# A two-layer streaming encoder on one core: cross attention moves from one woven stream into the other, and the large tiles become pages of one pool

## The chip, the core and the metric

The kernel runs on one core of one Trainium2 chip. PE (TensorE) multiplies matrices, DVE (VectorE), ACT (ScalarE) and POOL (GpSimd) work on elements, and SP (SyncE) issues nearly all DMAs. Each of the five takes its instructions in the order in which they stand in its queue. The metric is the device time of one execution in microseconds; the time before is the median of three runs.

## What is computed

Two layers run over 1,024 prompt tokens and 32 sample tokens, both with the same weights. A layer of the reference, cut to its steps:

```python
z = split_in(rms_norm(x, g[N_MIX_PRE]), p['w_in'])           # one projection, 1024 -> 2720
a = diff_finish(blocked_queries(... diff_attention ...))      # 8 heads, two softmaxes each
b = band_prompt(z['b_q'], z['b_k'], z['b_v'], p['rel'])       # 4 heads, own chunk and 8 before it
c = blocked_queries(... mla_attention ...)                    # 4 heads, latent keys and values
x = x + rms_norm(concat([a, b, c]) @ p['w_out'], g[N_MIX_POST])
x = x + rms_norm(cross_attention(rms_norm(x, g[N_X_PRE]), mk, mv, w_xq, w_xo), g[N_X_POST])
f = (silu(conv(h @ w_gate)) * (h @ w_up)) @ w_down            # h = rms_norm(x, g[N_F_PRE])
x = x + rms_norm(f, g[N_F_POST])
```

The sample tokens do the same against given caches of keys and values, and the new keys, values and states are outputs as well.

## The kernel before

Activations lie transposed, 128 features on the partitions and tokens along the row. The 1,056 tokens are two halves (`HW = (544, 512)`; the 32 sample tokens belong to half 0), and each half is two groups of 256 or 288 columns. Every large product is done with three matmuls (`mm3`, L214 to L216): operands are split into a rounded high part and the rest, and high times high, high times rest and rest times high are summed. So each weight tile of 128 x 1024 is loaded into `wr`, rounded by ACT (`hi`, L112) into `wh`, and its rest taken by POOL (`lo`, L131) into `wl`; `get` runs this feed two tiles ahead, in an order that `make_feed` writes out.

The work of a half in a layer has four parts. `project` is the norm and the input projection; `attend` is the attention of groups A, B and C, whose units pass through a pipeline of steps (scores, weights, transpose, product); `cross` is the output projection w_out, the cross attention and the norms around them; `ffn` is the gated MLP, two weight tiles of w_gate and w_up to one of w_down. In names, stage(l, h) is layer l, half h. Inside `cross`, `outputs` brings in the attention's results from DRAM, the w_out loop copies its products out by ACT at L1423, and what follows is a chain: `queries` (norm, norm, w_xq, L1457), `attention` over 256 memory tokens (L1475, L1518), `rest` (w_xo, norm, the MLP's norm). The sums of squares of a norm are added by DVE and POOL at L243 and summed over partitions by a matmul with ones at L251. The MLP's first gate product is evacuated by DVE at L1585, its last sums are added at L1645.

All parts are generators, which yield the PE time that they have just issued, or a negative number for a time in which others should be issued. `weave` runs attention as the main stream with one other stream as its fill:

```python
self.weave(self.attend(0, 1), w1, tail(0, 0), tail_cost(0, 0), 350.0 / w1)
self.weave(first(1), w0, tail(0, 1), tail_cost(0, 1), 250.0 / w0)
self.weave(self.attend(1, 1), w1, tail(1, 0), tail_cost(1, 0), 350.0 / w1)
self.emit(tail(1, 1))
```

Here `tail(l, h)` is cross, ffn and the next layer's project of one half, and `first(l)` is attend(l, 0) with the sample tokens' attention spread through it. So cross(l, h) and ffn(l, h) follow each other in one stream, and the last half of the last layer runs alone. A scheduler then takes the instructions in about the order of issue, and fixes where each stands on its engine and which buffer a tile gets. Buffers come from one pool with a count for each tag: `X=16, y=8, op=4, V=3, e0=2, e1=1, s=3` for the large ones, among them X for split activations, op for keys, V for values, e for softmax weights and s for their transposes.

## Time and profile before

| | |
|---|---|
| median of 3 runs (lowest to highest) | 3822.57 us (3818.94 to 3830.19) |
| the profiled execution | 3822.06 us |
| its span, first to last instruction | 3820.3 us |
| busy in the span: PE, POOL, DVE, ACT | 3322.2, 2079.6, 2034.8, 1833.2 us |
| mean granted clock of PE | 0.921 |

Busy time is a union of an engine's instructions. The granted clock is a share of the full 2.4 GHz. A wait is put down to the work that ended last before it.

### The profile page before, as it was taken

To read this page: it belongs to the slowest core of one execution; us is meant where nothing else is said; L and a number is where in the kernel's file an instruction comes from. 1 tells how busy PE (TensorE), PEld (TensorE's weight loads), DVE (VectorE), ACT (ScalarE), POOL (GpSimd) and SP (SyncE) were. 2 spreads that over 40 slices of the span, in tenths; PEclk is the share of its full clock that TensorE was granted. 3 is DMA by queue.
4 is the path that set the end of the run, shared out by engine and by line. 5 is a ranking of instruction groups with operands and counts; after the bars stand their busy time and mean duration, and the time that the engine had idled before them with its cause. 6 is when DMAs were issued, how large, how long until landed. Compare 5 with 4: busy or idle time off the path is not lost.

```text
span 3820.3 us, 65949 instructions
## 1 busy us (share of the span) xinstructions
PE 3322.2 (87%) x24536; PEld 3138.7 (82%) x24536; DVE 2034.8 (53%) x4627; ACT 1833.2 (48%) x3926; POOL 2079.6 (54%) x1868
## 2 busy tenths in 40 slices
PE   7989977689999798778999999776999996679997
PEld 7979876589999797768999888766999996669997
DVE  4464437855555633574544543487555553554444
ACT  4464556654444535574434344565544444543332
POOL 6454455456555644545666554545655554556564
PEclk9989988899999998878999989878999998789998
DMA  7657643223233455333333365323324323122222
GB/s 243 200 173 227 213 143 105 87 79 104 82 105 107 145 197 161 121 95 100 108 96 108 97 209 187 112 75 96 105 82 122 107 90 105 61 76 91 84 89 78
DMA packets 246791, 464.78 MB, mean 122 GB/s; under 512 B 42544, under 2 KB 136136, under 8 KB 246472
## 3 DMA queue, kind: packets, MB, share of 16 engines
q1 hardware_dynamic: 244024, 457.07, 38.3%
q8 instruction: 194, 3.18, 0.4%
q0 software_dynamic: 2448, 3.51, 0.3%
q14 instruction: 125, 1.02, 0.1%
HBM read 365.93 MB, written 97.66 MB: 121 GB/s over the span
## 4 chain that ended last, share of the span: by engine, by line
PE 63%; DVE 16%; ACT 6%; DMA 5%; issue 5%; POOL 4%; SPq 1%; POOLq 0%; DVEq 0%; ACTq 0%
PE ps_g L214 17%; PE ps_g L215 17%; PE ps_g L216 17%; DVE gt L1609 3%; PE ps_g L547 2%; PE ps_g L251 2%; PE ps_g L618 1%; DVE y L441 1%; PE ps_g L617 1%; POOL wl L131 1%; ACT wh L112 1%; DVE s L129 1%; DVE X L409 1%; DVE zn L243 1%; DVE sm L690 1%
## 5 line engine op out<-in xcount | busy, mean ns | idle before, releaser
L214 PE MATMUL ps_g<-X,wh 128*128 128x256 f32 (+1 forms) x5120 | 1486.6, 292 | 34.3 <-ACT X L112 19.0
L215 PE MATMUL ps_g<-X,wh 128*128 128x256 f32 (+1 forms) x5120 | 1479.7, 290 | 8.0 <-POOL X L131 5.0
L216 PE MATMUL ps_g<-X,wl 128*128 128x256 f32 (+1 forms) x5120 | 1470.2, 288 | 1.8 <-POOL wl L131 1.8
L131 POOL TENSOR_TENSOR wl<-wr,wh 128x1024 fp32r<-128x1024 f32 x416 | 991.5, 2389 | 572.9 <-ACT wh L112 554.5
L214 PEld LDWEIGHTS ps_g<-X,wh 128*128 128x128 f32 x5120 | 982.6, 192 | 46.8 <-ACT X L112 23.7
L215 PEld LDWEIGHTS ps_g<-X,wh 128*128 128x128 f32 x5120 | 981.6, 192 | 12.7 <-POOL X L131 6.3
L216 PEld LDWEIGHTS ps_g<-X,wl 128*128 128x128 f32 x5120 | 977.2, 191 | 2.6 <-POOL wl L131 2.0
L112 ACT ACTIVATE wh<-wr 128x1024 fp32r<-128x1024 f32 x416 | 432.8, 1052 | 796.4 <-PE ps_g L215 540.4
L214 PE MATMUL ps_g<-hs,wh 128*128 128x256 f32 (+1 forms) x1424 | 412.0, 298 | 41.5 <-DVE y L1645 35.3
L215 PE MATMUL ps_g<-hs,wh 128*128 128x256 f32 (+1 forms) x1424 | 411.8, 292 | 5.6 <-POOL hs L131 5.6
L216 PE MATMUL ps_g<-hs,wl 128*128 128x256 f32 (+1 forms) x1424 | 408.9, 290 | 0.0
L640 ACT ACTIVATE e<-ps_sc,sm 128x640 f32<-128x640 f32 (+7 forms) x384 | 278.7, 727 | 139.8 <-DVE e L706 52.7
L1609 DVE SCALAR_TENSOR_TENSOR gt<-gt,cst,gt 128x32 f32<-128x32 f32 (+3 forms) x264 | 273.0, 1051 | 89.3 <-ACT gt L1604 88.4
L1645 DVE TENSOR_TENSOR y<-y,ps_g 128x256 f32<-128x256 f32 (+1 forms) x640 | 261.7, 422 | 107.6 <-PE ps_g L216 106.0
L214 PEld LDWEIGHTS ps_g<-hs,wh 128*128 128x128 f32 x1424 | 271.4, 195 | 56.5 <-DVE y L1645 41.6
L215 PEld LDWEIGHTS ps_g<-hs,wh 128*128 128x128 f32 x1424 | 277.6, 195 | 7.8 <-POOL hs L131 6.7
L216 PEld LDWEIGHTS ps_g<-hs,wl 128*128 128x128 f32 x1424 | 278.0, 195 | 0.3
L129 DVE TENSOR_TENSOR s<-ps_g,s 128x512 fp32r<-128x512 f32 (+3 forms) x384 | 197.9, 533 | 147.2 <-ACT s L112 122.6
L1585 DVE TENSOR_TENSOR gt<-ps_g,r 128x256 f32<-128x256 f32 x176 | 74.6, 424 | 361.3 <-PE ps_g L216 354.7
L112 ACT ACTIVATE s<-ps_g 128x512 fp32r<-128x512 f32 (+3 forms) x384 | 173.4, 473 | 134.0 <-PE ps_g L547 132.2
L547 PE MATMUL ps_g<-ident,e 128*128 128x128 f32 x1104 | 181.8, 293 | 49.1 <-DVE e L706 29.3
L702 POOL TENSOR_SCALAR e<-e,sm,small 128x128 f32<-128x128 f32 (+7 forms) x128 | 115.9, 905 | 195.2 <-DVE sm L700 187.3
(246 smaller groups left out, 5366.5 us busy)
## 6 DMA issues: line engine op xcount, KB each, us to landing
wr<-i_w_in SPq DMA_DIRECT2D x88, 512.0 KB
wr<-i_w_gate SPq DMA_DIRECT2D x88, 512.0 KB
wr<-i_w_up SPq DMA_DIRECT2D x88, 512.0 KB
wr<-i_w_down SPq DMA_DIRECT2D x88, 512.0 KB
wr<-i_w_out SPq DMA_DIRECT2D x32, 512.0 KB
qt<-aq SPq DMA_DIRECT2D x192, 64.0 KB
V<-av SPq DMA_DIRECT2D x24, 512.0 KB
op<-ak SPq DMA_DIRECT2D x96, 128.0 KB
```

The lines of the kernel that those rows point to most:

```text
L112: nc.scalar.activation(out, in_, AF.Copy)
L129: nc.vector.tensor_sub(out, in_, h)
L131: nc.gpsimd.tensor_sub(out, in_, h)
L214: nc.tensor.matmul(out, wh, xh, start=(i == 0), stop=False)
L215: nc.tensor.matmul(out, wh, xl, start=False, stop=False)
L216: nc.tensor.matmul(out, wl, xh, start=False, stop=(i == n - 1))
L251: nc.tensor.matmul(p, ones, a, start=(i == 0), stop=(i == len(acc) - 1))
L547: self.nc.tensor.transpose(q[:, i * 128 : i * 128 + 128], e[:, c : c + 128], self.ident)
L640: self.nc.scalar.activation(e[:, :n], sc, AF.Exp, bias=m, scale=-1.0, accum_out=z)
L702: nc.gpsimd.tensor_scalar(e[:, :n], e[:, :n], sm[:, 3:4], self.nlam[:, l : l + 1], op0=ALU.mult, op1=ALU.mult)
L1609: nc.vector.scalar_tensor_tensor(cv[:, a:b], gp[:, a + o - e : b + o - e], conv_col(f, tap), cv[:, a:b], op0=ALU.mult, op1=ALU.add)
L1645: nc.vector.tensor_add(y[m][:, cols(g)], y[m][:, cols(g)], p)
```

## The change

Three things are done. `weave` goes, and two streams run side by side in `par`, the routine that already ran the groups of a half next to each other: `dense` has the projections and the MLPs of all halves, `latent` has the attention of a half, then its cross stage, then the attention of the next half. `paced` and `slowed` turn the latent stream's yields into PE time and waits, with a span for each attention (`SPANS`). Conditions replace the fixed order: an MLP waits for its cross stage (`"done" in F`), attention for its projection (`d.ready`), the first cross stage for the memory's keys (`known`). The memory's keys are made between the projections of the two halves. Second, the large tags become one, `pg`, with 26 pages of 1,088 columns; keys, values, softmax weights, their transposes, split activations and w_down's sums all take pages. Third, the weights of the cross stage leave the feed: they are loaded and split into pages of their own.

```diff
+SPANS = (220.0, 480.0, 400.0, 380.0)
+NPG = 26
-    BUFS = dict(X=16, y=8, wr=2, wh=3, wl=3, op=4, V=3, e0=2, e1=1, s=3, zn=3, ob=2, st=3, qt=2, sm=8,
-                strip=2, sst=1, qb=1, sg=1, kn=2, vn=1, sel=3, hs=3, gt=3, u=1, xr=2, r=1)
+    BUFS = dict(pg=NPG, wr=2, wh=3, wl=3, zn=4, ob=2, st=3, qt=2, sm=8,
+                strip=2, sst=1, qb=1, sg=1, kn=2, vn=1, sel=3, hs=3, gt=3, u=1, xr=2, r=2)
...
-            for name, n in (("w_out", KT), ("w_xq", 2), ("w_xo", 2)):
-                for i in range(n):
-                    add(name, l, i)
...
+    def half_tiles(self, dt=F32):
+        pages = [self.t("pg", dt) for _ in range(KT // 2)]
+        return [pages[k // 2][:, (k % 2) * HW[0] : (k % 2 + 1) * HW[0]] for k in range(KT)]
...
-            return a[:, 0], a[:, 1]
-        return [self.t("s", F32R)[:, :2048].rearrange("p (k c) -> p k c", k=8) for _ in range(2)]
+        return [[self.t("pg", F32R)[:, :1024].rearrange("p (k c) -> p k c", k=4) for _ in range(-(-n // 4))] for _ in range(2)]
...
-                            k = head[c] = self.t("op", F32R)
+                            k = head[c] = self.t("pg", F32R)[:, :1024]
...
-                                e = w[c] = self.t("e%d" % c)
+                                e = w[c] = self.t("pg")[:, :1024]
...
         for p in range(4):
+            yield lambda: d.ready[h] > p
             yield from self.attn_a(l, p, h, *d.zA[p], d.od)
...
+    def paced(gen, total, pe, span):
+        for x in gen:
+            if callable(x):
+                yield x
+            else:
+                yield pe * x / total
+                if x:
+                    yield -(span - pe) * x / total
+    def slowed(gen, k):
+        for x in gen:
+            yield x
+            if not callable(x) and x > 0:
+                yield -k * x
...
-        y = [self.t("y") for _ in range(KT)]
+        ws = split(load("w_out", 0))
+        y = self.half_tiles()
         for m in range(KT):
-            w = self.get(("w_out", l, m))
+            if m + 1 < KT:
+                raw = load("w_out", m + 1)
             for g in G:
                 p = self.ps("g")[:, : width(g)]
-                self.unit(w, O[g], p)
+                self.unit(ws, O[g], p)
...
+            done.add("first" if g == G[0] else "second")
             ys = [t[:, cols(g)] for t in y]
             for z in self.postnorm(y2, l, 3, ys, g, ys, d.x2):
                 yield z
-            done.add("first")
+            del y2
+            yield lambda: "second" in done
...
+        F["done"] = True
...
+        def dense():
+            x1 = self.first_load(1)
             yield from p0
-            yield from self.first_norm(1)
+            yield from self.first_norm(1, x1)
+            del x1
+            yield from self.mem_setup()
+            known.append(True)
             yield from self.project(0, 1)
-            yield from self.mem_setup()
...
+            for l, h in order:
+                yield lambda: "done" in F[l, h]
+                yield from self.ffn(l, h, F[l, h])
+                if l + 1 < DEPTH:
+                    yield from self.project(l + 1, h)
...
+        def latent():
+            for l, h in order:
+                a = self.attend(l, h)
+                if h == 0:
+                    a = self.spread(a, w[0], self.samples(l), 46)
+                yield from self.paced(a, w[h], (110.0, 150.0)[h], spans[l, h])
+                yield lambda: bool(known)
+                yield from self.slowed(self.cross(l, h, F[l, h]), 1.0)
...
-        self.weave(first(0), w0, opening(), self.project_cost(0) * 19 / 22 + self.project_cost(1) + 25, 250.0 / w0)
-        self.weave(self.attend(0, 1), w1, tail(0, 0), tail_cost(0, 0), 350.0 / w1)
-        self.weave(first(1), w0, tail(0, 1), tail_cost(0, 1), 250.0 / w0)
-        self.weave(self.attend(1, 1), w1, tail(1, 0), tail_cost(1, 0), 350.0 / w1)
-        self.emit(tail(1, 1))
+        self.emit(self.par(latent(), dense()))
```

Every line of the file moves: `mm3` is L217 to L219 after the change, the sums with ones L254.

What the change does to the order shows at three places. The first is PE at the end of ffn(1,0). Names are tile<-operands; `hs,wh` is a product of w_down, `X,wh` (before) and `pg,pg` (after) is one of the cross stage, `ident,e` a transpose of attention's weights. Before:

```order
L214 MATMUL ps_g_36254<-hs_35960,wh_35963 128x288
L215 MATMUL ps_g_36254<-hs_35960,wh_35963 128x288
L216 MATMUL ps_g_36254<-hs_35960,wl_35964 128x288
L214 MATMUL ps_g_36254<-hs_36021,wh_36024 128x288
L215 MATMUL ps_g_36254<-hs_36021,wh_36024 128x288
L216 MATMUL ps_g_36254<-hs_36021,wl_36025 128x288
L251 MATMUL ps_g_36270<-zn_36151,ones 128x256 x2
L547 MATMUL ps_g_36296<-ident,e_6095_36212 128x128 x4
L547 MATMUL ps_g_36301<-ident,e_6095_36212 128x128 x3
```

The same engine and place after:

```order
L217 MATMUL ps_g_36622<-hs_36400,wh_36403 128x256
L218 MATMUL ps_g_36622<-hs_36400,wh_36403 128x256
L219 MATMUL ps_g_36622<-hs_36400,wl_36404 128x256
L217 MATMUL ps_g_36622<-hs_36519,wh_36522 128x256
L218 MATMUL ps_g_36622<-hs_36519,wh_36522 128x256
L219 MATMUL ps_g_36622<-hs_36519,wl_36523 128x256
L217 MATMUL ps_g_36630<-pg_35728,pg_36566 128x256
L218 MATMUL ps_g_36630<-pg_35732,pg_36566 128x256
L219 MATMUL ps_g_36630<-pg_35728,pg_36567 128x256
```

Before, the last w_down products are followed by attention's last units and w_out comes after them; after, products of w_out in cross(1,1) stand between those of w_down, and attention's units stand ahead.

The second place is PE inside cross(0,1), after its queries: `ident,gt` (before) and `ident,pg` (after) are transposes of the cross attention's weights, `ps_sc<-op,qt` and `s,V` are scores and products of attention(1,0), which runs beside it before. Before:

```order
L547 MATMUL ps_g_18846<-ident,gt_18731 128x128 x2
L617 MATMUL ps_g_18897<-s_18774,V_18168 128x256
L618 MATMUL ps_g_18897<-s_18774,V_18168 128x256
L617 MATMUL ps_g_18897<-s_18774,V_18168 128x128
L618 MATMUL ps_g_18897<-s_18774,V_18168 128x128
L683 MATMUL ps_sc_18909<-op_18507,qt_18697 128x256
L683 MATMUL ps_sc_18909<-op_18503,qt_18697 128x256
L683 MATMUL ps_sc_18951<-op_18819,qt_18823 128x384
```

The same engine and place after:

```order
L219 MATMUL ps_g_18142<-pg_18068,pg_17879 128x256
L575 MATMUL ps_g_18212<-ident,pg_18198 128x128 x4
L575 MATMUL ps_g_18221<-ident,pg_18198 128x128 x4
L1537 MATMUL ps_sc_18230<-pg_18171,pg_18007 128x256
L1538 MATMUL ps_sc_18230<-pg_18171,pg_18008 128x256
L1536 MATMUL ps_sc_18230<-pg_18171,pg_18007 128x256
L1537 MATMUL ps_sc_18230<-pg_18171,pg_18007 128x256
L1538 MATMUL ps_sc_18230<-pg_18171,pg_18008 128x256
```

Attention's scores and products no longer stand there: all rows are of the cross stage, its queries' last product, transposes and scores.

The third place is SP near the end of project(1,0) after the change, where before only the feed's weights, w_out among them, went to `wr`:

```order
L108 DMA wr_17440<-i_w_gate 128x1024
L108 DMA o_pe<-gt_17058 32x544
L108 DMA kp_118<-hs_17059 32x2x544
L108 DMA pg_17353<-i_w_out 128x1024
L108 DMA pg_17467<-i_w_out 128x1024
L108 DMA wr_17530<-i_w_gate 128x1024
L108 DMA wr_18801<-i_w_up 128x1024
```

The loads of cross(0,1)'s w_out go to pages, and the first gate and up weights of ffn(0,1) are loaded to `wr` beside them.

## Rows read from the trace of the kernel before

**Rows 1.** The page: span, busy time by engine, the chain that ended last.

```profile
span 3820.3 us, 65949 instructions
...
PE 3322.2 (87%) x24536; PEld 3138.7 (82%) x24536; DVE 2034.8 (53%) x4627; ACT 1833.2 (48%) x3926; POOL 2079.6 (54%) x1868
...
PE 63%; DVE 16%; ACT 6%; DMA 5%; issue 5%; POOL 4%; SPq 1%; POOLq 0%; DVEq 0%; ACTq 0%
```

**Rows 2.** Lines L1423 and L1585 (from 3300 on): count, duration, first and last start.

```profile
L1423 ACT ACTIVATE y<-ps_g x64: 362/384/410, 547.6 to 3267.7; 128x256 f32<-128x256 f32 x48, 128x288 f32<-128x288 f32 x16
...
L1585 DVE TENSOR_TENSOR gt<-ps_g,r x44: 418/425/426, 3388.7 to 3755.1; 128x256 f32<-128x256 f32 x44
```

**Rows 3.** Busy time by stage: window, its length, each engine, clock, DMA share.

```profile
core 0: us, PE busy (x) PEld busy (x) DVE busy (x) ACT busy (x) POOL busy (x), PEclk, DMA share, GB/s
0.00:505.00 505.00, 448.70 (x3321) 415.44 (x3321) 263.54 (x704) 266.33 (x666) 250.52 (x269) 0.96 0.66 209
598.00:781.00 183.00, 115.97 (x664) 98.51 (x664) 153.57 (x343) 118.03 (x293) 88.89 (x99) 0.78 0.30 89
781.00:1270.00 489.00, 475.31 (x3615) 458.40 (x3614) 271.99 (x634) 215.94 (x376) 286.56 (x236) 1.00 0.32 97
1571.00:1747.00 176.00, 120.03 (x707) 99.76 (x707) 134.14 (x376) 110.10 (x327) 87.82 (x117) 0.73 0.37 109
1747.00:2185.00 438.00, 426.40 (x3434) 413.28 (x3433) 211.00 (x466) 180.47 (x316) 264.51 (x214) 0.98 0.32 100
2466.00:2652.00 186.00, 119.50 (x662) 101.70 (x661) 156.63 (x349) 119.26 (x297) 88.57 (x100) 0.75 0.33 93
2652.00:3168.00 516.00, 505.86 (x3825) 488.76 (x3824) 292.66 (x683) 235.75 (x420) 293.77 (x242) 0.99 0.32 97
3168.00:3224.00 56.00, 23.89 (x117) 19.75 (x116) 25.68 (x46) 22.71 (x58) 23.06 (x26) 0.70 0.42 123
3224.00:3268.00 44.00, 43.87 (x365) 43.33 (x363) 4.15 (x6) 20.43 (x44) 24.17 (x18) 1.00 0.34 106
3268.00:3388.00 120.00, 62.89 (x353) 54.22 (x351) 74.20 (x142) 63.49 (x178) 62.74 (x71) 0.70 0.20 62
3388.00:3794.00 406.00, 387.78 (x3151) 385.12 (x3150) 172.87 (x319) 144.55 (x206) 245.46 (x177) 0.97 0.24 80
```

**Rows 4.** Waits in the lone tail: in total, times, longest.

```profile
PE ps_g L251 <- DVE zn L243: 38.1, 5, 17.7
```

**Rows 5.** Windows in the projections, columns as before.

```profile
256.00:428.00 172.00, 169.80 (x1339) 157.56 (x1339) 83.15 (x229) 86.89 (x216) 83.10 (x84) 0.98 0.61 196
1310.00:1460.00 150.00, 148.74 (x1167) 146.52 (x1166) 51.12 (x91) 61.04 (x124) 74.49 (x56) 1.00 0.52 174
2235.00:2365.00 130.00, 126.88 (x1027) 124.99 (x1026) 31.93 (x51) 49.20 (x97) 65.31 (x41) 0.97 0.64 212
```

**Rows 6.** Windows: last value product to first gate; ends of the lone tail.

```profile
703.00:781.00 78.00, 46.06 (x248) 39.47 (x247) 61.16 (x133) 47.60 (x114) 35.72 (x38) 0.74 0.31 96
1684.00:1747.00 63.00, 40.10 (x237) 35.17 (x236) 50.54 (x123) 37.49 (x108) 31.47 (x39) 0.70 0.38 116
3300.00:3388.00 88.00, 51.45 (x279) 44.31 (x276) 50.83 (x103) 50.06 (x143) 42.96 (x53) 0.71 0.17 54
3320.00:3388.00 68.00, 36.95 (x183) 31.58 (x183) 40.95 (x84) 38.49 (x108) 31.55 (x39) 0.67 0.17 56
```

**Rows 7.** POOL's split of weight tiles: ffn(1,1), then ffn(1,0).

```profile
L131 POOL TENSOR_TENSOR wl<-wr,wh x62: 2360/2394/2412, 3399.3 to 3778.0; 128x1024 fp32r<-128x1024 f32 x62
...
L131 POOL TENSOR_TENSOR wl<-wr,wh x48: 2367/2400/3119, 2748.5 to 3115.9; 128x1024 fp32r<-128x1024 f32 x48
```

**Rows 8.** Waits of SP's queue and of ACT over the span.

```profile
SPq L102 <- DVE y L1645: 94.2, 23, 13.2
...
ACT wh L112 <- DMA wr<-i_w_gate: 124.9, 27, 5.5
```

More of the change, by code (lines that the diff above doesn't have):

```diff
@@ L345, in mem_setup @@
         for l in range(DEPTH):
-            pages = [self.t("X", F32R) for _ in range(8)]
+            pages = [self.t("pg", F32R) for _ in range(4)]
             mn = []
@@ L384, in gain, with prenorm @@
         return self.cst[:, c : c + 1]
-    def prenorm(self, xs, l, which, w, out, lo=("pool",)):
+    def prenorm(self, xs, l, which, w, out, pages, lo=("pool",)):
         nc = self.nc
@@ L400, in prenorm, with prenorm_late @@
         yield -4
-    def prenorm_late(self, xs, l, which, w, r, out):
+    def prenorm_late(self, xs, l, which, w, r, out, pages):
         nc = self.nc
-        xh, xl = self.chunk_pages(w)
+        xh, xl = pages()
         for k in range(KT):
@@ L1187, in c_queries @@
         yield -2
+        pages = [self.t("pg", F32R).rearrange("p (x c) -> p x c", x=2) for _ in range(2)]
         for g, r in zip(G, rs):
@@ L1266, in par @@
                 now += y
-    @staticmethod
-    def weave(main, total, fill, cost, pace):
-        credit, left, wait = 0.0, cost, 0.0
-        x = 0.0
-        for y in fill:
-            if y < 0:
-                wait -= y
-                while wait > 0 and x is not None:
-                    x = next(main, None)
-                    if x is not None:
-                        total -= x
-                        wait -= x * pace
-            elif y > 0:
-                wait = min(0.0, wait + y)
-                credit += y * max(total, 0.0) / max(left, y)
-                left -= y
-                while credit > 0 and x is not None:
-                    x = next(main, None)
-                    if x is not None:
-                        credit -= x
-                        total -= x
-        for _ in main:
-            pass
     def layer(self, l):
@@ L1530, in rest @@
             yield lambda: "attention" in done
[L1531 removed]
+            if g == G[0]:
+                wraw = [load("w_xo", k) for k in range(2)]
+                yield -4
+                wx.extend(split(raw) for raw in wraw)
+                F["r"] = self.t("r")
+                yield -4
+            else:
                 yield lambda: "first" in done
             w = width(g)
[L1534 to L1539 removed]
+            y2 = self.chunk_tiles(w)
             for m in range(KT):
```

235 lines of the change are left out of this document (136 added, 99 removed).

## The prediction

> **What bounds the kernel now.** I read the page first, then busy time by stage, then the waits inside the worst stage. PE is busy for 3322 of 3820 us and holds most of the chain that ended last, DVE 16% of it [rows 1]. The share is an average over two kinds of stage. I cut the span at the lines that mark them: the last copy of a w_out product (L1423) ends a cross stage's dense half, the first gate product (L1585) starts an MLP. For layer 1, half 1 these stand at 3268 and 3389 [rows 2]. In the windows [rows 3] the reader is to see three things.
>
> First, the MLP stages are nearly full: PE 475 of 489, 426 of 438, 506 of 516 and 388 of 406 us, at a granted clock of 0.97 to 1.00. Second, four stretches are not: 598 to 781, 1571 to 1747, 2466 to 2652 and 3268 to 3388, 665 us together, which I call tails. They run from w_out's end to the first gate product: norm, queries, softmax over the memory, w_xo, two norms. PE is busy for half to two thirds of them and gets a clock of 0.70 to 0.78, a mean of the levels 1.2 and 2.4 GHz. In the last tail, where nothing else is left to run, PE waits 38 us in five waits for the sums of squares that feed a norm (L251 after L243) [rows 4]: a chain of dependent steps, not a lack of throughput. Third, the other three tails take 56 to 66 us more than the last one's 120. They hold attention work, and there DVE is the busy engine: 154 of 183 us against 74 of 120. So attention fills PE's gaps in the tail, but pays for it on DVE.
>
> **The change, costed.** The operations stay: PE has 23,999 matmuls in both orders (the trace of before has 24,536 records of them), SP 1,843 DMAs before and 1,841 after. So the sum is one of places: which matmuls of the new order stand where, times the rate of the nearest stage of before. I counted PE's order of both kernels.
>
> Rates, window over matmuls in the order of before. MLP stages with attention: 489 us for 3,729 (131 ns), 438 for 3,498 (125), 516 for 3,900 (132); the MLP alone 406 for 3,173 (128) [rows 3]. Clean projection: 150, 130 and 172 us for 1,167, 1,027 and 1,339 records, 127 to 129 ns [rows 5]. w_out alone: 44 us for 365 records, 121 ns [rows 3]. Opening: 505 us for the 3,223 matmuls ahead of the first cross stage.
>
> The places in the order of after:
> 1. Up to the last matmul of project(0,1) stand 3,631. The first 3,223 at the opening's price, 505; the 408 more are w_out of cross(0,0) and its first queries, at 128 ns: 52. Sum 557. mem_setup moves ahead of project(0,1), at no cost: the same matmuls.
> 2. Then 305 matmuls of cross(0,0) with only four of attention among them, up to the first gate. In the lone tail the last 279 records took 88 us, from 3300 on [rows 6]. Half 0 has the sample's cross attention too: from the last value product to the gate 78 us, against 63 without it [rows 6], so 15 more. 103.
> 3. ffn(0,0), 3,968 with attention(0,1): 131 ns, 520.
> 4. project(1,0), 1,777 with attention's end and three quarters of w_out: 128 ns, 227, and 20 for the norms ahead of it, which attention covers in part. 247.
> 5. cross(0,1): 96 matmuls of w_out and its whole tail follow the last of project(1,0), 420 in all, four of them attention. 12 + 120 = 132.
> 6. ffn(0,1), 3,858: 131 ns, 505.
> 7. project(1,1), 1,700, with nearly all of w_out and the queries of cross(1,0): 128 ns and 10 for norms, 228.
> 8. cross(1,0): 175 are left when the projection ends; the last 183 records of the lone tail took 68 us [rows 6], and 15 for the sample. 83.
> 9. ffn(1,0), 4,576, with attention(1,1) and three quarters of cross(1,1)'s w_out: 132 ns, 604.
> 10. cross(1,1): 97 of w_out and the whole tail, 416, nothing beside them: 132.
> 11. ffn(1,1) as before, 406, and from 3794 to the end 26.
>
> Sum 3,543. Where the gain comes from: tails with 665 us become 426 (103 + 120 + 83 + 120); the starts of the cross stages, like 3168 to 3224 with PE at 24 of 56 us [rows 3], now lie beside MLP or projection matmuls; against this, attention that stood in the tails is paid at 131 ns in the MLPs.
>
> What is not in it: whether DVE takes that attention as easily. By the tails, attention cost it 79, 60 and 82 us over the lone tail's 74: 222. If all fits between the MLP's own DVE work, which is 173 of 406 us alone and 293 of 516 with attention [rows 3], it costs nothing; if half does not, 111. I take 35, near the lower end, since the MLP stages with the most attention ran at 132 ns against 128 without. That gives 3,578; the profiled execution took 3822.06 for a span of 3820.3, and the runs' median is 3822.57, so 3,580 for the metric.
>
> The page pool itself I cost at nothing: 26 pages of 1,088 columns replace tiles of nearly the same total. Its cover is the order, which lets other matmuls pass while a page is waited for; where the order and the chip disagree, an engine waits in its queue, which is the second rival.
>
> A rule that speaks against the change: POOL's split of a weight tile has a median of 2394 ns in the MLP alone and 2400 ns with attention beside it, though one of 48 took 3119 [rows 7]; so by these rows mixing costs POOL nothing. The Trainium skill, "SBUF — State Buffer", section "Who interferes with whom", says that a DVE instruction with two SBUF inputs and a GpSimd one that reads SBUF lock each other out. This trace shows it at most in that one of 48; if each of the 198 splits in the three mixed MLPs met such a 0.7 us wait on PE's path, the sum would be 139 us higher, about 3,720, inside the third rival below.
>
> **Rivals.**
> A. *The tails vanish.* PE could take MLP work in them, if the order on the chip were fed so. Then the four tails cost their 353 records each at 128 ns, 181 in place of 426: about 3,335. Against it: the order has no other matmuls there, since the dense stream waits for the cross stage's result and attention follows cross in one stream. Chance 0.08.
> B. *Slower: page loads hold the weights up.* SP issues in one line. Before, attention's key and value loads waited for their own small pools; now keys, values and the cross weights need one of 26 pages, and behind a load that waits stands the MLP's next weight. The MLP holds 8 pages of inputs and 4 of sums, a cross stage up to w_out's end 8 of inputs, 4 of sums and 3 or more of weights: 27 in all. Nearest row: SP waited 94.2 us in 23 waits for y to be read (4.1 each); and ACT waited 124.9 us for gate weights in 27 waits, longest 5.5, already [rows 8]. The three mixed MLPs have 198 weights. One in three late by 4.1 us on PE's path costs 271: 3,850. It decides from 59 such waits on (242 us). For it: the page count. Against it: the order was made with the pool's size, so most waits stand as a different order already. Chance 0.12.
> C. *DVE is the bound where attention went.* The 222 us are not hidden: 3,543 + 222, about 3,767; from 111 (3,656) on I count it as this case. For it: DVE at 84% in the tails; in ffn(1,0) 1,108 attention matmuls now stand where 728 stood. Against it: DVE at 57% in that stage. Chance 0.18, nearly all of it still faster than before.
>
> **How the numbers follow.** The forecast has 0.62 and its own range is 3,470 to 3,690 (no crowding and cheaper norm gaps at one end, half of the 222 at the other). A has 0.08, C 0.18 (up to 3,810), B 0.12 (above that). From 3,470 to 3,790 leaves out A, B and C's last part, some 0.2. Within 0.3% of before, 11 us, is about what this measurement can tell from no change: it gets 0.04, from the border of B and C. Slower is B's 0.12, faster the rest, 0.84.
>
> **What would show it.** Right: a stretch without MLP or projection matmuls ahead of each MLP's first gate product, near 103, 132, 83 and 132 us, with clocks near 0.70; no low clock at the starts of the cross stages; MLP stages with attention near 131 ns. DVE in ffn(1,0) near 70% and PE waiting for it would be C. Waits of SP for pages, followed by ACT waiting for gate or up weights and PE for ACT or POOL, would be B. MLP matmuls inside the tails would be A. The prediction falls most easily on step 1, whose rate comes from the stretch that is reordered most, and on steps 4 and 7, where a clean projection's rate is taken for a mixed one: 10 ns a matmul in these three, 7,108 together, is 71 us.

## The result and the profile after

The changed kernel takes 3725.75 us (median of 3 runs, 3719.39 to 3728.03) against 3822.57: the ratio is 0.974, 95% interval 0.971 to 0.977. It became faster by 97 us, where 242 had been forecast. A second set of runs of the same kernel gave 3718.87 us and 0.9724 (0.9706 to 0.9742); the experiments below are read against that one, by their ratios to the kernel before.

The page of the changed kernel, to be held against [rows 1]: span, busy time, chain that ended last.

```profile
span 3725.5 us, 66150 instructions
...
PE 3266.1 (88%) x24536; PEld 3099.4 (83%) x24536; DVE 2073.0 (56%) x4627; ACT 1836.3 (49%) x3926; POOL 2080.5 (56%) x1868
...
PE 64%; DVE 14%; ACT 7%; DMA 6%; issue 4%; POOL 4%; SPq 1%; POOLq 0%; ACTq 0%; DVEq 0%
```

PE's busy time fell by 56 us although it does the same work: in the traces 356 us of it stood at the lower of the two clock levels (1.2 GHz) before and 268 us after, 88 us less, against 30 us more at the full one; the mean granted clock is 0.928 for 0.921. Then busy time by stage. I matched each matmul of the order to its record in the trace and cut where the first or the last matmul of a stage starts, so the windows answer to the prediction's steps: step 1 is the first four rows together, steps 2 to 11 one row each (11 without the last 24 us).

```profile
core 0: us, PE busy (x) PEld busy (x) DVE busy (x) ACT busy (x) POOL busy (x), PEclk, DMA share, GB/s
0.00:273.00 273.00, 230.22 (x1675) 212.11 (x1676) 152.03 (x429) 141.52 (x368) 129.51 (x153) 0.95 0.66 208
273.00:384.20 111.20, 83.28 (x482) 67.17 (x481) 61.76 (x180) 63.55 (x171) 53.46 (x65) 0.80 0.55 165
384.20:547.10 162.90, 158.84 (x1273) 156.24 (x1274) 35.64 (x66) 67.25 (x142) 81.31 (x59) 0.98 0.52 175
547.10:627.60 80.50, 60.87 (x421) 56.38 (x420) 43.95 (x66) 38.88 (x94) 45.04 (x39) 0.81 0.47 151
627.60:728.60 101.00, 58.84 (x330) 50.31 (x328) 60.06 (x117) 58.61 (x159) 50.16 (x65) 0.69 0.21 67
728.60:1289.60 561.00, 528.69 (x3950) 503.95 (x3948) 383.21 (x895) 285.71 (x528) 337.58 (x276) 0.97 0.37 112
1289.60:1544.30 254.70, 241.13 (x1822) 233.19 (x1821) 97.28 (x179) 123.77 (x269) 125.07 (x101) 0.96 0.51 163
1544.30:1678.90 134.60, 72.35 (x438) 62.57 (x438) 79.75 (x159) 73.52 (x196) 69.89 (x79) 0.71 0.23 72
1678.90:2222.60 543.70, 504.75 (x4053) 479.38 (x4051) 327.55 (x835) 276.04 (x603) 327.04 (x314) 0.97 0.40 124
2222.60:2446.80 224.20, 214.82 (x1717) 210.58 (x1716) 96.83 (x134) 104.83 (x232) 133.49 (x106) 0.98 0.47 158
2446.80:2519.80 73.00, 36.21 (x197) 30.29 (x196) 42.13 (x93) 44.80 (x119) 36.44 (x45) 0.69 0.29 98
2519.80:3147.20 627.40, 610.17 (x4592) 584.33 (x4590) 419.21 (x969) 339.11 (x651) 363.76 (x301) 0.99 0.38 113
3147.20:3288.90 141.70, 72.10 (x434) 63.02 (x432) 88.98 (x170) 71.08 (x192) 72.70 (x84) 0.69 0.25 77
3288.90:3701.80 412.90, 393.56 (x3180) 389.88 (x3178) 174.44 (x321) 146.80 (x211) 246.84 (x178) 0.97 0.24 79
```

| step | predicted | measured |
|---|---|---|
| 1 opening, to the last matmul of project(0,1) | 557 | 627.6 |
| 2, 5, 8, 10: the four tails | 103 + 132 + 83 + 132 = 450 | 101.0 + 134.6 + 73.0 + 141.7 = 450.3 |
| 3, 6, 9: the mixed MLPs | 520 + 505 + 604 = 1,629 | 561.0 + 543.7 + 627.4 = 1,732.1 |
| 4, 7: projections of layer 1 | 247 + 228 | 254.7 + 224.2 |
| 11 the lone MLP and the end | 432 | 436.6 |
| crowding, put on the sum | 35 | in the rows above |

The tails came out as predicted in their sum, with clocks of 0.69 to 0.71, and the misses sit in two places: 71 us in the opening and 103 us in three stages in which PE is 93 to 97% busy. A stage that is nearly full and still longer than its price points to the price. Here is the kernel before once more, cut in the same way: the opening to its 3,223rd matmul, and its three mixed MLPs from their first matmul to their last, then the end of the first of them.

```profile
0.00:521.60 521.60, 463.71 (x3427) 429.70 (x3428) 268.23 (x717) 272.00 (x675) 260.89 (x274) 0.95 0.66 209
774.70:1305.80 531.10, 500.59 (x3740) 480.20 (x3738) 301.29 (x691) 235.20 (x422) 309.10 (x256) 0.98 0.34 103
1740.70:2219.70 479.00, 457.21 (x3568) 437.93 (x3566) 242.59 (x538) 202.47 (x376) 289.50 (x242) 0.96 0.34 105
2648.50:3187.50 539.00, 520.08 (x3906) 501.11 (x3905) 307.31 (x707) 244.82 (x439) 305.49 (x253) 0.98 0.32 98
1270.00:1305.80 35.80, 18.98 (x100) 15.93 (x97) 29.28 (x57) 18.31 (x45) 22.54 (x21) 0.76 0.66 201
```

The prediction had divided 489, 438 and 516 us [rows 3] by matmuls that really took 531, 479 and 539, and 505 by matmuls that took 522. Its windows began 4 to 6 us behind the first matmul that they counted and ended 20 to 36 us ahead of the last. What fell between is above all the end of each MLP, where a norm runs and PE is busy for half of the time (19 of 36 us in the last row).

### The profile page after: what moved, and what is told of

Same layout as the page of the kernel before. It is cut to its first block, busy times and chain, and to the rows that moved or that the text cites. A ratio compares the mean times of both kernels' runs of the same rounds, so it can differ in the third digit from the quotient of the medians.

```text
span 3725.5 us, 66150 instructions
## 1 busy us (share of the span) xinstructions
PE 3266.1 (88%) x24536; PEld 3099.4 (83%) x24536; DVE 2073.0 (56%) x4627; ACT 1836.3 (49%) x3926; POOL 2080.5 (56%) x1868
## 4 chain that ended last, share of the span: by engine, by line
PE 64%; DVE 14%; ACT 7%; DMA 6%; issue 4%; POOL 4%; SPq 1%; POOLq 0%; ACTq 0%; DVEq 0%
PE ps_g L217 17%; PE ps_g L218 17%; PE ps_g L219 16%; DVE gt L1676 4%; PE ps_g L575 3%; DVE pg L469 2%; PE ps_g L651 2%; PE ps_g L650 1%; PE ps_g L254 1%; PE ps_sc L716 1%; DMA xr<-x 1%; ACT wh L118 1%; DVE pg L412 1%; POOL wl L137 1%; DVE zn L246 1%
## 5 line engine op out<-in xcount | busy, mean ns | idle before, releaser
L217 PE MATMUL ps_g<-pg,wh 128*128 128x256 f32 (+1 forms) x4352 | 1260.2, 290 | 20.2 <-ACT pg L118 17.1
L218 PE MATMUL ps_g<-pg,wh 128*128 128x256 f32 (+1 forms) x4352 | 1251.9, 288 | 5.3 <-POOL pg L137 3.9
L219 PE MATMUL ps_g<-pg,wl 128*128 128x256 f32 (+1 forms) x4352 | 1246.2, 286 | 0.0
L137 POOL TENSOR_TENSOR wl<-wr,wh 128x1024 fp32r<-128x1024 f32 (+1 forms) x368 | 885.6, 2411 | 457.7 <-ACT wh L118 437.2
L217 PEld LDWEIGHTS ps_g<-pg,wh 128*128 128x128 f32 x4352 | 828.4, 190 | 30.2 <-ACT pg L118 20.2
L218 PEld LDWEIGHTS ps_g<-pg,wh 128*128 128x128 f32 x4352 | 826.6, 190 | 10.0 <-POOL pg L137 5.3
L219 PEld LDWEIGHTS ps_g<-pg,wl 128*128 128x128 f32 x4352 | 822.9, 189 | 0.2
L118 ACT ACTIVATE wh<-wr 128x1024 fp32r<-128x1024 f32 (+1 forms) x368 | 383.4, 1053 | 555.7 <-PE ps_g L218 402.9
L217 PE MATMUL ps_g<-hs,wh 128*128 128x256 f32 (+1 forms) x1424 | 417.4, 299 | 45.3 <-DVE pg L1712 39.7
L219 PE MATMUL ps_g<-hs,wl 128*128 128x256 f32 (+1 forms) x1424 | 408.2, 289 | 0.0
L673 ACT ACTIVATE pg<-ps_sc,sm 128x640 f32<-128x640 f32 (+7 forms) x384 | 278.0, 729 | 125.0 <-DVE sm L724 73.8
L217 PEld LDWEIGHTS ps_g<-hs,wh 128*128 128x128 f32 x1424 | 271.2, 193 | 64.6 <-DVE pg L1712 48.7
L1712 DVE TENSOR_TENSOR pg<-pg,ps_g 128x256 f32<-128x256 f32 (+1 forms) x640 | 260.3, 422 | 89.4 <-PE ps_g L219 87.2
L135 DVE TENSOR_TENSOR pg<-ps_g,pg 128x512 fp32r<-128x512 f32 (+2 forms) x448 | 225.7, 518 | 101.7 <-ACT pg L118 99.3
L219 PEld LDWEIGHTS ps_g<-hs,wl 128*128 128x128 f32 x1424 | 275.5, 193 | 0.2
L217 PE MATMUL ps_g<-pg,pg 128*128 128x256 f32 (+1 forms) x768 | 229.0, 299 | 5.2 <-ACT pg L118 5.2
L219 PE MATMUL ps_g<-pg,pg 128*128 128x256 f32 (+1 forms) x768 | 225.2, 295 | 1.1 <-POOL pg L137 1.0
```

The lines of the kernel that those rows point to most:

```text
L118: nc.scalar.activation(out, in_, AF.Copy)
L135: nc.vector.tensor_sub(out, in_, h)
L137: nc.gpsimd.tensor_sub(out, in_, h)
L217: nc.tensor.matmul(out, wh, xh, start=(i == 0), stop=False)
L218: nc.tensor.matmul(out, wh, xl, start=False, stop=False)
L219: nc.tensor.matmul(out, wl, xh, start=False, stop=(i == n - 1))
```

## The experiments

Three theories went in. *Places*: full stages keep their rates, and the miss is in stretches with too little for PE to do. *Crowding*: attention moved into the MLPs delays them through DVE. *Pages*: the prediction's rival B. Each kernel below is the changed kernel with the edit shown. The first gate is the first product of w_gate in ffn(0,0). Stage lengths of the changed kernel are those of its second profile, unless rows of the table above are meant. Rates are given for a matmul, or for a record of the trace, which has 24,536 records for the 23,999 matmuls.

**dve_twice.**
```diff
             self.hi("act", oh, q3)
             self.lo("dve", ol, q3, oh)
+            self.lo("dve", ol, q3, oh)
```


> The changed kernel with one DVE step of attention issued twice: the subtraction that makes the low part of each transposed weight tile (some 400 instructions at a median of 0.55 us, about 200 us of DVE work more, the same values written again). Theories. Places: the full stages run at the rates of before, and what the predicted sum missed are two stretches with too little for PE to do, the ends of the three mixed MLPs and the opening. Crowding: attention that was moved into the MLPs delays them through DVE. Places expects under 40 us more in all and about 134 ns a matmul record inside the mixed MLPs as now. Crowding expects more than 100 us more, most of it inside ffn(0,0), ffn(0,1) and ffn(1,0).

Measured: 3783.59 us, 0.989 (0.9869 to 0.9911), 64 us more by the ratios. The page counts 384 more DVE instructions and 159.6 us more busy time than after, so 0.4 us is paid for each us of DVE work, more than places allowed and less than crowding asked. Most is paid in the MLPs: ffn(0,0), ffn(0,1) and ffn(1,0) are 19, 6 and 31 us longer than in the second profile of the changed kernel. The windows below are the middle of ffn(0,0), first of the changed kernel, then of this one, 134.6 ns a record and 138.8. DVE work is not free there even at 73% busy. The doubled step also lies between a transpose and the product that needs it, so this run does not tell a crowded DVE from a longer chain.

```profile
780.00:1220.00 440.00, 427.43 (x3268) 412.73 (x3266) 301.29 (x711) 221.52 (x390) 265.82 (x209) 1.00 0.34 104
```
```profile
780.00:1220.00 440.00, 418.82 (x3171) 403.08 (x3170) 321.11 (x750) 214.76 (x377) 261.07 (x205) 0.99 0.34 102
```

In the kernel before, the middle of the same stage ran at 135.4 ns a record (390 us for 2,881):

```profile
830.00:1220.00 390.00, 379.08 (x2881) 364.96 (x2879) 211.54 (x503) 165.34 (x280) 228.85 (x186) 1.00 0.32 98
```

DVE was 54% busy there and is 68% busy after the change, and a record costs the same, though more of the records are attention's. So DVE work has a price, but the attention that the change moved did not raise the rate here. Rival C had two signs, DVE near 70% in ffn(1,0) and PE waiting for it there. The first came, 419 of 627 us or 67% in the table above; the second did not, as PE's longest group of waits between 2555 and 3100 us is this:

```profile
PE ps_g L217 <- DVE pg L1712: 8.8, 8, 1.8
```

**npg24.**
```diff
-NPG = 26
+NPG = 24
```


> The changed kernel with 24 pages in place of 26. PE's order of matmuls stays the same, so only waits for pages can change. Places expects the time within 0.5% (19 us) of the changed kernel. The rival of the prediction, page loads that hold up SP and so the weights, expects 60 us more or worse, with ACT waiting longer for gate and up weights.

Measured: 3712.04 us, 0.9708 (0.969 to 0.9725), no slower than the changed kernel. Each stage has the same number of matmuls, though some hundreds of the 23,999 places in the order differ, and every stage is within 4 us. Nor did rival B's own sign come, ACT waiting longer for gate weights: 67.0 us for 124.9 before [rows 8]. PE has one long group of waits for pages, three of 20 to 22.5 us in the three tails after which an attention follows: its first scores wait for keys there, ahead of the last norm's sums. The lone tail has no such scores, and at the same place it waits 22.1 us for the norm itself. In the other three the norm's sums found their inputs at about the time at which the keys came (waits of up to 0.2 us). So rival B has no part in the miss that these runs show.

```profile
ACT wh L118 <- DMA wr<-i_w_gate: 67.0, 19, 5.3
PE ps_sc L716 <- DMA pg<-ak: 64.8, 3, 22.5
PE ps_g L254 <- ACT st L244: 22.1, 1, 22.1
```

**mem_late** and **mem_beside.** The first moves one call, and the wait for the keys (cut here) to behind w_out inside the cross stage; the second gives the memory's keys a stream, and their weights go to pages. The feed's order follows in both.
```diff
-            yield from self.mem_setup()
-            known.append(True)
             yield from self.project(0, 1)
+            yield from self.mem_setup()
+            known.append(True)
```


> The changed kernel with the memory's keys made after project(0,1), as before the change, and the wait for them moved from the head of the first cross stage to behind its w_out. Ahead of the first matmul of project(0,1) then stand 1,599 matmuls in place of 1,980; between the last of project(0,1) and the first gate of ffn(0,0) 633 in place of 305. Places expects project(0,1) to end near 505 us (628 now), and the first gate near 660 (729 now): 50 to 80 us faster. If the opening is bound by its loads, or by attention's own chain of steps, the first gate moves by under 15 us.

```diff
-            yield from self.mem_setup()
-            known.append(True)
+            started.append(True)
             yield from self.project(0, 1)
...
-        self.emit(self.par(latent(), dense()))
+        self.emit(self.par(latent(), memory(), dense()))
```


> The changed kernel with the memory's keys made in a third stream of its own, which starts when the second half's first norm is done and runs beside project(0,1); its four weight tiles a layer leave the feed and go to pages. So its chain of small steps has projection matmuls beside it. Price of w_out of cross(0,0): it moves out of project(0,1), since attention ends later (matmuls ahead of project(0,1) 1,597 for 1,980, in it 1,620 for 1,651, behind it up to the first gate 719 for 305). If the opening is slow because the memory's chain stands alone: project(0,1) starts near 298 us, takes 1,620 at 0.136 us (220), then w_out 46 and the tail 101: first gate near 665 to 680, some 50 to 60 us faster in all. If the opening is slow because of its loads or of attention's own steps, beside which the memory's chain costs nothing by itself: first gate within 15 us of 729.

Measured: 3714.9 us, 0.9714 (0.9697 to 0.9731), and 3720.76 us, 0.973 (0.9709 to 0.9752): no change. Windows of mem_beside, project(0,1) and then up to the first gate:

```profile
295.40:530.10 234.70, 218.12 (x1692) 206.26 (x1691) 92.75 (x214) 117.84 (x283) 117.31 (x98) 0.96 0.60 199
530.10:720.10 190.00, 115.39 (x750) 103.97 (x748) 83.37 (x164) 92.14 (x233) 93.22 (x101) 0.78 0.23 76
```

project(0,1) ends 98 us earlier than in the changed kernel, and the stretch without dense work after it is 89 us longer; mem_late does the same (530 and 193 us). The first gate is at 720 and 723 us, against 724 in the second profile of the changed kernel. Work that fills one hole in the opening is missed in the next, so counting the exposed matmuls, as places did, priced nothing here.

**span_short** and **short_norms.**
```diff
-SPANS = (220.0, 480.0, 400.0, 380.0)
+SPANS = (220.0, 400.0, 340.0, 320.0)
```


> The changed kernel with shorter spans for attention: 220, 400, 340, 320 us of PE time in place of 220, 480, 400, 380, so that cross stages start earlier. Matmuls with no MLP or projection beside them, ahead of the four MLPs: 305, 132, 117, 295 in place of 305, 420, 175, 416. Places expects these 467 to fall from about 0.32 us each to 0.13, some 90 us, and up to 20 us more at the ends of ffn(0,0) and ffn(0,1), where w_out now stands: near 3,620 to 3,640. Crowding expects no gain: attention then runs a fifth denser in MLPs where DVE is at 65 to 77% already. Pages expects a loss, since w_out's pages are asked for while the MLP still holds its own.

Measured: 3691.63 us, 0.9657 (0.9638 to 0.9676), 26 us faster by the ratios where places wanted 90. The four exposed stretches, those ahead of an MLP's first gate product with no MLP or projection matmuls in them, did shrink from 101, 133, 73 and 142 us (second profile of the changed kernel) to 100, 51, 44 and 90, by 163 us together. But the stages between them grew by 134 us, where the 467 matmuls that they took in cost 64 at 138 ns. Two windows of ffn(0,0), its middle and its end, where the outputs of cross(0,1) stand beside:

```profile
721.00:1250.00 529.00, 517.81 (x3892) 495.41 (x3891) 373.92 (x886) 284.76 (x527) 305.12 (x259) 0.99 0.38 113
1250.00:1348.70 98.70, 62.01 (x422) 55.88 (x420) 54.33 (x109) 47.46 (x111) 46.58 (x43) 0.81 0.39 112
```

The middle costs 135.9 ns a record, the end 234. PE's longest waits from 1300 to 1365 us, as the view of waits gives them:

```profile
PE ps_g L254 <- ACT zn L244: 31.8, 2, 31.5
PE ps_g L217 <- ACT pg L118: 12.9, 1, 12.9
```

One sum over the partitions for the norm in `outputs` stands in PE's queue ahead of MLP products and waits for 31.5 us. The next kernel issues that sum later.

```diff
         accs = [self.sum_squares([a for _, a in xs[i : i + 2]], w) for i in (0, 2)]
-        yield -2
+        yield -8
         rs = [self.inv_rms([a], self.bd, 64.0, w) for acc in accs for a in acc]
```


> The kernel with shorter spans (220, 400, 340, 320), and in outputs the matmul that sums the squares of attention's results is issued 8 us of PE time behind its squares in place of 2. PE takes its matmuls in order, so one norm matmul that waits for its inputs holds up the MLP's matmuls behind it; with the shorter spans such a wait at the end of ffn(0,0) was 31.5 us and one at the end of ffn(0,1) 8.1. If order stalls are what the denser MLPs cost, these waits fall by 6 us each or more and the time by 15 to 35 us against the kernel with the shorter spans alone (3,692). If DVE crowding is what they cost, it stays within 8 us.

Measured: 3678.07 us, 0.9618 (0.96 to 0.9637), 13.6 us better in the medians: between the two bounds. The wait of 31.5 us is gone, but at the same place the MLP's own norm now waits:

```profile
PE ps_g L254 <- DVE zn L246: 26.7, 2, 19.4
```

The stage is as long as with span_short (626 and 628 us). ffn(0,1) and ffn(1,0) are 22 and 25 us shorter, against 45 us more in the exposed stretches ahead of ffn(1,0) and ffn(1,1). The edit also moved matmuls: 96 and 20 fewer stand in those two MLPs, 26 and 20 more in those two stretches. So PE does stall behind a waiting norm, but taking one such wait out of a stage that has two chains in it showed the other, and where the 13.6 us came from is not told apart from the moved matmuls.

**three_streams.**
```diff
-                yield lambda: bool(known)
-                yield from self.slowed(self.cross(l, h, F[l, h]), 1.0)
+                attended.append((l, h))
...
-        self.emit(self.par(latent(), dense()))
+        self.emit(self.par(crossing(), latent(), dense()))
```


> The changed kernel with attention and cross attention in two streams of their own: the attention of a half may start as soon as the cross attention's value products of the half before are issued, so it runs beside the rest of the tail, as before the change. Matmuls ahead of the four MLPs' first gate without MLP or projection matmuls: 335, 282, 196, 315 in place of 305, 420, 175, 416, of them 33, 16, 56 and 0 of attention. Places expects about 190 fewer exposed ones at 0.2 us gained each, less 10 to 20 for DVE work of attention in the tail: 20 to 30 us faster. If attention in a tail costs what it did before the change (56 to 66 us a tail more than the lone one for some 200 matmuls, 0.3 us each), the gain is under 10 us.

Measured: 3750.43 us, 0.9808 (0.9789 to 0.9827), slower than the changed kernel by 32 us; both expectations missed. The four exposed stretches fell from 448 to 388 us, but what lies between them grew by 95 in the profiled runs. ffn(0,0) and ffn(0,1) took in 148 and 132 matmuls for 20 us each, their price; ffn(1,0) took in 48 for 24 us; project(1,0) has 11 fewer and took 21 us more (262.6 for 241.4):

```profile
1329.60:1592.20 262.60, 234.94 (x1787) 229.73 (x1786) 103.30 (x163) 120.02 (x265) 136.88 (x109) 0.94 0.48 155
```

Its two longest waits, where the changed kernel's longest in this stage is 5.3 us:

```profile
PE ps_g L217 <- DVE hs L135: 11.1, 1, 11.1
PE ps_g L254 <- DVE zn L246: 10.3, 1, 10.3
```

The second is a norm's sum again; the order has 54 matmuls of cross(0,1)'s queries, with their norms, in this stage, where the changed kernel has none.

**tail_loads, xr_three, all_loads, xr_six.** The chain of work at the end of ffn(0,0) in the changed kernel, in order of time (start, us, what), pointed to loads of x:

```profile
1273.40 5.55 DMA xr<-x
1279.08 1.01 POOL pg L470
...
1281.57 4.27 DMA xr<-x
```

```diff
+            x1 = self.chunk_tiles(w)
+            for i in range(KT):
+                self.dma(x1[i], d.xin[i, :, span(g)])
...
-            yield from self.postnorm(ys, l, 1, d.xin, g, ys)
+            yield from self.postnorm(ys, l, 1, x1, g, ys)
+            del x1
```


> The changed kernel with the stage's input x, which the norm behind w_out adds, loaded to two or three pages a group at the head of the queries, where before the change and after it came through the two xr buffers in the middle of the norm. In the chain of work of the lone tail (3147 to 3290 us) the six xr loads hold 19.0 us. If the tail is a chain of dependent steps whose length is what is paid, each of the four tails gets 10 to 19 us shorter and the time falls by 40 to 75 us. If something else in the tail ends last (the queries' weights, DVE's own work), it falls by under 15 us.

```diff
-                strip=2, sst=1, qb=1, sg=1, kn=2, vn=1, sel=3, hs=3, gt=3, u=1, xr=2, r=2)
+                strip=2, sst=1, qb=1, sg=1, kn=2, vn=1, sel=3, hs=3, gt=3, u=1, xr=3, r=2)
```


> The changed kernel with three xr buffers in place of two. Since the change two streams load through them at the same time: outputs (attention's results) and the norm at an MLP's end, which 1252 to 1302 and 2175 to 2225 us show as 50 us with PE at 0.4 to 0.7 busy, where before the change these ends took some 36 us. If that sharing is what made the ends longer: 10 to 15 us less at each of the two ends, 20 to 30 us in all. If the chain is long by itself: under 8 us.

all_loads does the same as tail_loads in `finish`, where the MLP's norm is:
```diff
+            x2 = self.chunk_tiles(width(g))
+            for i in range(KT):
+                self.dma(x2[i], d.x2[i, :, span(g)])
             yield from down_units(k, ws, g)
-            yield from self.postnorm(ys, l, 5, d.x2, g, ys, d.x3)
+            yield from self.postnorm(ys, l, 5, x2, g, ys, d.x3)
+            del x2
```
xr_six has `xr=6` and `NPG = 24`.

> As tail_loads, and the same for the norm at an MLP's end: its x is loaded to pages before the last w_down products. The chain of work from 2170 to 2232 us has 6.4 us of such loads, from 1246 to 1300 us 9.8 us. If chains are what is paid at the ends of the MLPs too, 6 to 10 us less at each of the four ends than with tail_loads alone, 20 to 40 us. If attention and outputs hold PE up there, under 10 us.

> The changed kernel with six xr buffers and 24 pages, the same order of matmuls. If the two streams' sharing of xr is a queue in which each load waits for the one before, more buffers take out what three leave: another 10 to 20 us below the kernel with three (3,690). If three were enough for two streams, within 8 us of it.

Measured: tail_loads 3719.99 us, 0.9735 (0.9715 to 0.9755), nothing; xr_three 3689.88 us, 0.9659 (0.9643 to 0.9675); all_loads 3696.36 us, 0.9675 (0.966 to 0.9689); xr_six 3679.79 us, 0.9624 (0.9609 to 0.9639). By the ratios a third xr buffer is worth 25 us, all_loads 19, and six buffers 38 (32 against the kernel that has 24 pages too). Waits for loads of x before the change, in the changed kernel (second profile), and with three buffers:

```profile
POOL y L442 <- DMA xr<-x: 33.8, 21, 5.2
DVE y L442 <- DMA xr<-x: 23.8, 16, 5.5
```
```profile
POOL pg L470 <- DMA xr<-x: 38.6, 19, 5.1
DVE pg L470 <- DMA xr<-x: 36.6, 21, 5.6
```
```profile
POOL pg L470 <- DMA xr<-x: 25.2, 13, 3.7
DVE pg L470 <- DMA xr<-x: 17.1, 13, 3.6
```

With six the view lists none. With as many matmuls in each stage, and nearly the same order, the first gate then stands at 710 us (three) and 714 (six) in place of 724, and mixed MLPs are 6 to 14 us shorter each, but for ffn(1,0) with six. The four tails keep 447 and 439 us in place of 448: in the lone tail of tail_loads the same 22 us waits ahead of the gate stand as without it. So the tail's loads lay beside another chain of the same length. With three buffers 14 us of the gain lie ahead of the first gate and only 6 and 4 at the ends of ffn(0,0) and ffn(0,1), where the expectation had put all of it: its sum came true, its place did not. Nor is it shown that two streams sharing the buffers made the price, since the kernel before already waited 58 us for these loads (the changed one 75) and was not run with a third buffer.

**combined, combined_xr3, combined_dense, open_150.** combined is short_norms with all_loads; combined_xr3 has `xr=3` besides; combined_dense is that with the first edit below, and `yield -16` in outputs; open_150 is the changed kernel with the second.
```diff
-SPANS = (220.0, 400.0, 340.0, 320.0)
+SPANS = (220.0, 380.0, 320.0, 300.0)
```
```diff
-SPANS = (220.0, 480.0, 400.0, 380.0)
+SPANS = (150.0, 480.0, 400.0, 380.0)
```

> All that has paid so far: shorter spans, the norm of outputs issued later (together 3,678 us), and the loads of all_loads. If the gains are apart from each other: 3,678 less the gain of all_loads, some 3,580 to 3,620. If shorter chains only uncover the next wait in PE's order: 3,640 or above.

> The combined kernel (3,652 us) with three xr buffers. Its norms no longer load x through xr, so only outputs does; if sharing between streams was the price, there is little left to gain: within 8 us. If outputs waits on its own loads (four tiles through two buffers), 10 to 20 us faster, at the starts of the cross stages.

> The combined kernel with three xr buffers, spans of 220, 380, 320, 300 and the norm of outputs 16 us later: matmuls with no MLP or projection beside them 335, 124, 119, 289 in place of 331, 140, 143, 315. Places: 70 fewer at 0.2 us, 10 to 15 us below combined_xr3. Crowding (by the doubled DVE step: 65 us for some 200 us of DVE work, 0.3 each): denser attention costs as much as that: no gain, or a loss of up to 10 us.

> The changed kernel with the first attention's span at 150 in place of 220 us, nothing else: more of it beside project(0,0), and 54 matmuls of the queries more beside project(0,1) (269 in place of 305 before the first gate). If the opening is set by where matmuls stand: first gate 7 to 12 us earlier than 724. If it is set by a chain that runs from project(0,0) through attention, outputs and the queries, whatever stands beside: within 5 us.

Measured: combined 3652.4 us, 0.9559 (0.9544 to 0.9574), the fastest, 1.7% below the changed kernel. Its gains added up: all_loads is worth 19 us alone and 23 on top of short_norms, by the ratios. The expectation's 3,580 to 3,620 had counted on a larger gain of all_loads, so a time above 3,640 does not show that a next wait was uncovered. combined_xr3 3653.23 us, 0.9555 (0.954 to 0.957): nothing left in the buffers. combined_dense 3666.95 us, 0.959 (0.9571 to 0.961): 14 us worse, all of it by the first gate (723 us for 709); after it the stretch to ffn(1,1)'s last matmul takes 2,926 us for 2,924, though 66 matmuls fewer are exposed. Ahead of the first gate the spans are the same in both, so the loss points to the later norm and what moved with it; PE has one wait of 26.3 us there, for a sum of the queries' norms, which combined_xr3 has not:

```profile
PE ps_g L254 <- DVE zn L246: 26.6, 2, 26.3
```

Behind it the 66 matmuls gave nothing, as crowding expected and places did not; norms that hold up PE's queue would look the same. open_150 3730.29 us, 0.9761 (0.9738 to 0.9784): no faster, and the first gate at 733 us is 9 us later, which neither expectation had; project(0,0) with the denser attention took 26 us longer (the first row of the changed kernel's table is its 273), more than the stages behind it gave back:

```profile
0.00:298.90 298.90, 249.78 (x1811) 227.92 (x1812) 166.21 (x492) 154.54 (x408) 136.12 (x171) 0.94 0.64 201
```

The page of combined, where PE's busy time is another 19 us lower and the span 77 (in the profiled runs), so most of this gain is idle time of PE that went:

```profile
span 3648.1 us, 66341 instructions
...
PE 3247.3 (89%) x24536; PEld 3088.2 (85%) x24536; DVE 2090.9 (57%) x4627; ACT 1831.4 (50%) x3926; POOL 2069.8 (57%) x1868
```

## Why the prediction was right in sign and wrong in size

Sign and place of the gain were right, its size was 2.5 times too large. By its own steps, against the profiled span of 3725.5 us and a sum of 3,578:

- **Tails (steps 2, 5, 8, 10): right.** 450 predicted, 450.3 measured, from the lone tail's rate and 15 us for the sample. That the sum agrees so closely is luck: cross(1,0) took 10 us less than its step and cross(1,1) 10 more.
- **"Rates, window over matmuls" (steps 3, 6, 9): the step that failed.** With the whole stages of before, 531.1 us for 3,729 matmuls, 479.0 for 3,498 and 539.0 for 3,900 (142.4, 136.9 and 138.2 ns in place of 131, 125 and 132), the 3,939, 3,856 and 4,576 matmuls from the first to the last of an MLP after the change come to 561 + 528 + 632 = 1,721 us; 1,732 were measured and 1,629 predicted. So some 92 of the 103 us are this division, and 11 are left for everything else, crowding and the xr buffers among it: 0, 16 and -5 us in the three stages. Step 6 had even taken the higher 131 in place of its own stage's 125, and was short all the same.
- **Step 1: failed in its size.** Of the 71 us, 17 are the same slip (505 us for what took 521.6). 25 are the time to the 3,223rd matmul, 547.1 us after against 521.6, and 28 the 408 matmuls behind it, 80.5 us in place of 52. "mem_setup moves at no cost" held in the net, by mem_late and mem_beside; that w_out and the queries run at a clean 128 ns beside project(0,1) did not: PE is 60.9 of 80.5 us busy there, at a clock of 0.81. The xr buffers hold 10 to 14 us of the opening. For the remaining 40 or so the runs name no cause, and it stays open. One lead: project(0,0) ended at 236 us with 1,397 matmuls done before, at 273 with 1,543 in the changed kernel and at 299 with 1,651 in open_150, so that attention packed in beside it came at some 0.25 us a matmul, against 0.16 in step 1; a wider first span was not tried. Of all edits only the buffers moved the first gate forward by more than 6 us; moving the memory's keys and starting attention earlier left it about where it was or later.
- **Steps 4 and 7, which the prediction had called weak, held** within 8 and 4 us; step 1, which it named first, did not.
- **The 35 us for crowding: not seen as a term.** The rates came from stages that already held attention, so it may have been paid twice; that is argued, not shown. That added DVE work has a price in the MLPs is shown (dve_twice, 0.4 us for each).
- **The pool at no cost: right** (npg24). That "the operations stay, so the sum is one of places" was incomplete: more xr buffers are worth 25 to 38 us with nearly the same places, and none of the rivals named them. Two streams that used them in turn now use them at once; how much of the price that made is not shown.
- **Rivals.** A: the tails did not vanish. B: nothing in npg24 or the waits speaks for it. C: the time lies in its range, but the rates above account for it without its 222 us; its signs came by half, and its size here is not told apart within the 11 us. The sum of about 3,720 by POOL's split lies near the measured time by luck: POOL's instructions lost some 20 us in the whole trace (last section).

Added up: 103 for the mixed MLPs, 71 for the opening, 8 for step 4, 5 for step 11, less 4 for step 7 and less the 35 that were not found: 148 us, and the span exceeds the sum by 147.5.

More overlap would not simply have brought the forecast gain. span_short and three_streams took 467 and 188 matmuls out of exposed stretches, and the kernel became 26 us faster and 32 slower; combined_dense took out 66 behind the first gate, and that part became 2 us slower. What was seen in these runs is that a chain of norms moved beside other work holds PE's queue up where its next sum is not ready; how much of the loss is that and how much DVE was not told apart.

## What to carry to other kernels

When a stage's rate is a window over a count, let both run from the same first to the same last instruction, and put the sum together for the kernel before first: the stretches that belong to no window show up as a remainder. A stage that moves beside another also moves its chain of waits, and on PE, whose queue ran in order here, these stopped the neighbour's work; count how long each of its inputs is late, not only how many matmuls are exposed. When two streams begin to run side by side, go through the small buffers that both use, not only the large ones, and give the kernel before the same buffers, to see what of the gain is new.

## What the hardware showed

The prediction looked only at POOL for the lock between POOL and DVE. It is mostly DVE that pays in these traces. The convolution of the lone MLP in the changed kernel, one shape (duration min/median/max in ns), and POOL's split beside it:

```profile
L1676 DVE SCALAR_TENSOR_TENSOR gt<-gt,cst,gt x44: 739/1680/2907, 3297.6 to 3666.0; 128x512 f32<-128x512 f32 x44
```
```profile
L137 POOL TENSOR_TENSOR wl<-wr,wh x63: 2377/2397/2412, 3296.9 to 3683.5; 128x1024 fp32r<-128x1024 f32 x63
```

The split keeps its time within 1.5%, the convolution takes up to four times its shortest. Counted over the trace, DVE instructions that took over 0.6 us more than the median of their line, tiles and shape are 75 before the change (88 us above the medians in all) and 122 after it (169 us). POOL was at work during every one, where it is during 55 and 59% of all DVE instructions; its instruction had begun first in all 75 and in 121 of the 122. POOL's own instructions were stretched as much 18 and 22 times (24 and 20 us). This agrees with the Trainium skill, "SBUF — State Buffer", section "Who interferes with whom": a DVE instruction with two SBUF inputs contends with a GpSimd one that reads SBUF, and which of the two was issued first decides who is blocked. Of the stretched ones 13 and 17 have one SBUF input alone, most of them casts, and of these that statement does not speak. DVE's busy time rose by 38 us with the same instructions. What those 80 us more of stretched work cost the kernel was not tried.
